# Two chunks of each feed-forward input projection as seven block products, on one Trainium2 core

## The chip, the cores and the metric

The kernel runs on one core of one Trainium2 chip. Its time is the device time of one execution in microseconds (us). Five engines work side by side, each with its own queue in order: PE multiplies matrices (PEld is the loading of its stationary operand), ACT (ScalarE), DVE (VectorE) and POOL (GpSimd) work element by element, SP issues the DMAs. PE writes to PSUM, eight banks of 128 x 512 floats; all other tiles lie in SBUF.

## What is computed

A trunk of two layers over 256 tokens of width 1024. Each layer is a feed-forward part (FFN), a token mixer and a second FFN, so there are four FFNs in the kernel. The change is in these:

```python
def swiglu_ffn(h, w_in, w_out):
    gate, up = jnp.split(h @ w_in, 2, axis=-1)        # w_in 1024 x 5632
    return (jax.nn.silu(gate) * up) @ w_out           # w_out 2816 x 1024

f = swiglu_ffn(rmsnorm(x, ffn1_norm_pre[i]), ffn1_w_in[i], ffn1_w_out[i])
x = x + 0.5 * rmsnorm(f, ffn1_norm_post[i])
```

The mixer between the FFNs (gated DeltaNet beside a causal convolution, with its own projections) is not touched.

## The kernel before, in words

**Products in three parts.** Every operand of a large product is kept as two float32r tiles, a high part `hi` and the rest `lo`, and `mm3` (L588) makes a product of three matmuls: high by high, high by low, low by high, all into one PSUM bank. Each matmul has a 128 x 128 stationary block of activations and 512 columns of weights.

**The weight stream.** `Stream` (L247) takes the weights in pieces of 128 x 1024 floats, 512 KB each. For each piece SP brings a `raw` tile (4 buffers), ACT copies it to `whi` (`high`, L276) and DVE or POOL makes `wlo` as raw minus whi (`low`, L280). `whi` and `wlo` have RING = 8 buffers each, so the preparation is at most eight pieces ahead of PE; `done` (L324) gives a buffer back when PE has used it and loads the next piece. In the FFNs all lows are DVE's; the set POOL (L75) names those of the mixer that GpSimd makes.

**The input projection** of an FFN, `proj_in` (L594), goes over 11 chunks of 512 columns: 256 gate columns and the 256 up columns that belong to them. A chunk is four pieces; each piece holds two of the eight 128-row steps of the inner dimension. For each of the two blocks of 128 tokens (tb 0, tb 1) a chunk takes 8 x 3 matmuls, 48 for the chunk, in two PSUM banks of tag `mm` (4 in all). At the start of an FFN (except the very first) chunks 0 and 1 are first done for tb 0 alone, while tb 1 is still being normalized.

**After a chunk**, `ev` (L699) takes the banks: ACT does the silu of the gate half, DVE multiplies by the up half. `fin` (L707) adds the job "ffn": two DVE transposes, four DMAs to DRAM, one DMA back, then ACT's high part and POOL's low part of the tile `act`, the operand of the output projection.

**The output projection**, `proj_out` (L655), has 22 steps of one piece each, 12 matmuls per piece, into four `mm` banks (two token blocks, two halves of 512 columns). The steps go by twos: two for tb 0, then the same two for tb 1. The last RING steps are finished first for tb 0, so that its normalization (`post`, L573, and `pre`, L449) runs beside tb 1.

**Order of the work.** PE runs in program order. `Lanes.tick` (L212) is called after every three matmuls or so and starts the next steps of the jobs, each after so many ticks as DELAY (L45) says. In the mixer the queues of DVE, POOL and ACT are put in the order of the program (`in_order`, `in_step`); in the FFNs of this kernel they are not, and the scheduler orders them by priorities. `Clocked` (L97) keeps an estimate of each engine's time while the program is written.

Of the kernel before, what the change touches and what calls it, by code (L numbers as in the profile page):

```python
# [76 lines left out]
CFG = dict(stat=1000, conv=50, ev=300, tok=4, st=4, post=-800, pre=1000, fin=None, turn=100, tokens=-100, glu=100, dec=200, dts=500, kt=300, vt=0, qt=50, inv=1000, sim=100, merge=-400, scan=50, norm=-800, onorm=-100, yt=-400, w=50, tails=4, ahead=1.5, lag=6, free=3, aheadp=3, lag2=3, bias=2, held=1)  # L77
# [4 lines left out]
        "yt0": "yt", "yt1": "yt"}  # L82
# [78 lines left out]
class Held:  # L161


    def __init__(self, eng, pe):
        self.eng, self.pe, self.tc = eng, pe, None

    def __getattr__(self, name):
        op = getattr(self.eng, name)

        def issue(*a, **k):  # L170
            r = op(*a, **k)  # L171
            if self.tc is not None:
                behind(self.tc, getattr(r, "ins", r), self.pe.last)
            return r
        return issue


class Lanes:
# [33 lines left out]
    def tick(self):  # L212
# [3 lines left out]
        if self.stream is not None:  # L216
            self.stream.tick()
# [28 lines left out]

class Stream:  # L247


    def __init__(self, tc, nc, pool, pieces, side, act, vec, gp):  # L250
        self.tc = tc
        self.act, self.vec, self.gp = act, vec, gp
# [4 lines left out]
        self.lanes, self.his, self.lows, self.still = None, [], [], True  # L257

# [4 lines left out]

    def load_one(self, parts=1):
        nc, src = self.nc, self.pieces[self.nload]
        i, n = self.nload, src.shape[-1]
        raw = self.pool.tile([P, D], F32, name="raw", tag="raw", bufs=4)
        hi = self.pool.tile([P, D], F32R, name="whi", tag="whi", bufs=RING)
        lo = self.pool.tile([P, D], F32R, name="wlo", tag="wlo", bufs=RING)
        for k in range(parts):  # L270
            c = slice(k * n // parts, (k + 1) * n // parts)
            nc.sync.dma_start(raw[:, c], src[:, c])
        self.loaded.append((hi, lo))
        self.nload += 1

        def high(c):  # L276
            with prio(self.tc, "w"):
                self.act.copy(hi[:, c], raw[:, c])
# [45 lines left out]
    def done(self):  # L324
        self.loaded[self.taken] = None
        self.taken += 1
        if not self.still:
            self.load()
# [1190 lines left out]
```

## Time and profile before

| what | value |
|---|---|
| time, median of 3 runs | 1345.21 us (1344.38 to 1346.62) |
| the profiled execution's own time | 1346.66 us |
| its span, first to last instruction | 1344.9 us |
| DMA | 273.77 MB, mean 204 GB/s |
| instructions | 20532 |

The page of the profile gives the busy time of each engine, then the span in 40 slices (one digit is a tenth of busy time), the DMA queues, the chain of work that ended last, and groups of instructions: line, engine, operation, output <- inputs, shapes, count, then busy us and mean ns of one, then the idle time just before them and what ended it. Lines 144, 171 and 124 are those of helpers that issue all of PE's, ACT's and DVE's or POOL's instructions, so groups are told apart by their tiles: `whi<-raw` is the high part of a weight piece, `wlo<-raw,whi` its low part, `ag<-mm` the gate, `way<-ag` the transposes, `act<-way` the parts of the output projection's operand, `xt<-tr` the splitting of the transposed input.

### The profile page before, as it was taken

The page shows a single profiled execution, that of the slowest core. Times are in us where ns is not written, and L with a number is a line of the kernel's source. Part 1 is how long each engine was busy: PE and PEld are TensorE (multiplying, and loading weights), DVE is VectorE, ACT ScalarE, POOL GpSimd, SP SyncE. Part 2 cuts the span into 40 slices and gives each one's busy share as a digit, 9 for nine tenths or more (in the row PEclk, how much of TensorE's full clock was granted, in tenths as well). Part 3 has the DMA queues.
Part 4 walks back from the last instruction along what each step waited for, and adds up shares of the span by engine and source line. Part 5 has one row for each costly group of instructions (what it writes and reads, how often), then busy time and mean ns, then how long its engine had stood idle before and what let it go on. Part 6 is the DMA issues. An engine that isn't in the chain of part 4 may idle for free.

```text
span 1344.9 us, 20532 instructions
## 1 busy us (share of the span) xinstructions
PE 1321.2 (98%) x7419; PEld 1120.4 (83%) x7419; DVE 931.6 (69%) x1592; ACT 731.8 (54%) x1175; POOL 451.2 (34%) x376
## 2 busy tenths in 40 slices
PE   9999999999999999999999999999999999999998
PEld 6888878998787878888888888799977878888886
DVE  6676455999975776665476654569999666766653
ACT  7555447676556545554455543577656564555541
POOL 0121016798853201111001110277997531011110
PEclk9999999999999999999999999999999999999999
DMA  8878746553643667776467776475536436477760
GB/s 280 280 238 254 260 159 199 179 187 120 192 155 126 232 212 235 253 260 220 151 228 268 258 253 190 129 236 168 183 122 206 154 133 233 158 267 261 260 210 34
DMA packets 115653, 273.77 MB, mean 204 GB/s; under 512 B 24768, under 2 KB 48352, under 8 KB 115552
## 3 DMA queue, kind: packets, MB, share of 16 engines
q1 hardware_dynamic: 115264, 272.40, 60.9%
q8 instruction: 58, 0.95, 0.3%
q14 instruction: 43, 0.35, 0.1%
q10 hardware_dynamic: 288, 0.07, 0.0%
HBM read 256.68 MB, written 15.75 MB: 203 GB/s over the span
## 4 chain that ended last, share of the span: by engine, by line
PE 77%; DVE 10%; POOL 3%; ACT 3%; issue 3%; DMA 3%; SPq 0%; POOLq 0%; DVEq 0%; ACTq 0%
PE mm L144 72%; DVE cacc L124 3%; PE gd L144 3%; DVE c L124 3%; DVE wlo L124 2%; POOL wlo L124 2%; PE tr L150 2%; DMA raw<-mw 2%; ACT whi L171 1%; DVE at L124 1%; POOL rk L124 1%; ACT dt L171 1%; DMA raw<-w2i 0%; DMA x<-x 0%; DMA raw<-w1i 0%
## 5 line engine op out<-in xcount | busy, mean ns | idle before, releaser
L144 PE MATMUL mm<-whi,xt 128*128 128x512 f32 (+1 forms) x2048 | 647.4, 391 | 4.2 <-ACT qT L171 2.2
L171 ACT CAST whi<-raw 128x1024 fp32r<-128x1024 f32 (+2 forms) x448 | 458.7, 1035 | 318.9 <-PE mm L144 177.8
L124 DVE TENSOR_TENSOR wlo<-raw,whi 128x1024 fp32r<-128x1024 f32 (+1 forms) x340 | 424.3, 1262 | 190.0 <-ACT whi L171 183.7
L144 PEld LDWEIGHTS mm<-whi,xt 128*128 128x128 f32 x2048 | 382.2, 188 | 85.0 <-DVE xt L124 3.1
L144 PE MATMUL mm<-wlo,xt 128*128 128x512 f32 (+1 forms) x1024 | 396.2, 387 | 0.1
L124 POOL TENSOR_TENSOR wlo<-raw,whi 128x1024 fp32r<-128x1024 f32 (+1 forms) x108 | 254.1, 2371 | 143.7 <-ACT whi L171 142.9
L144 PEld LDWEIGHTS mm<-wlo,xt 128*128 128x128 f32 x1024 | 192.7, 188 | 37.2 <-DVE wlo L124 0.8
L144 PE MATMUL mm<-whi,act 128*128 128x512 f32 x704 | 218.1, 390 | 0.0
L124 POOL TENSOR_TENSOR act<-way,act 128x512 fp32r<-128x512 f32 x44 | 81.2, 1845 | 393.8 <-ACT act L171 393.8
L124 DVE SCALAR_TENSOR_TENSOR cacc<-hT,pc,cacc 128x254 f32<-128x254 f32 (+28 forms) x464 | 179.3, 465 | 0.2
L144 PE MATMUL mm<-xt,whi 128*128 128x256 f32 x960 | 175.5, 285 | 0.8 <-ACT qT L171 0.6
L144 PEld LDWEIGHTS mm<-whi,act 128*128 128x128 f32 x704 | 132.2, 188 | 27.3
L144 PEld LDWEIGHTS mm<-xt,whi 128*128 128x128 f32 x960 | 149.4, 192 | 1.9 <-ACT qT L171 0.9
L144 PE MATMUL mm<-wlo,act 128*128 128x512 f32 x352 | 136.9, 389 | 0.0
L144 PE MATMUL mm<-xt,wlo 128*128 128x256 f32 x480 | 135.8, 283 | 0.0
L171 ACT ACTIVATE ag<-mm,rstd 128x256 f32<-128x256 f32 x88 | 41.8, 475 | 106.6 <-PE mm L144 76.3
L144 PEld LDWEIGHTS mm<-xt,wlo 128*128 128x128 f32 x480 | 92.0, 192 | 0.0
L124 DVE SCALAR_TENSOR_TENSOR ag<-mm,rstd,ag 128x256 f32<-128x256 f32 x88 | 42.4, 481 | 62.3 <-ACT ag L171 62.1
L144 PEld LDWEIGHTS mm<-wlo,act 128*128 128x128 f32 x352 | 66.1, 188 | 13.7
L124 POOL TENSOR_TENSOR rpost<-ss,exp 128x1 f32<-128x1 f32 x12 | 6.5, 541 | 194.0 <-DVE ss L124 194.0
L171 ACT ACTIVATE jk<-mm 128x512 f32<-128x512 f32 x24 | 14.4, 598 | 59.6 <-PE mm L144 59.6
L124 DVE SCALAR_TENSOR_TENSOR c<-mm,pc,c 128x255 f32<-128x255 f32 (+2 forms) x108 | 43.6, 473 | 2.6 <-ACT c L171 2.6
(187 smaller groups left out, 1139.2 us busy)
## 6 DMA issues: line engine op xcount, KB each, us to landing
raw<-mw SPq DMA_DIRECT2D x168, 512.0 KB, 3.7
raw<-w2i SPq DMA_DIRECT2D x88, 512.0 KB, 4.7
raw<-w1i SPq DMA_DIRECT2D x84, 512.0 KB, 4.8
raw<-w1o SPq DMA_DIRECT2D x44, 512.0 KB, 4.4
raw<-w2o SPq DMA_DIRECT2D x44, 512.0 KB, 4.2
way<-way SPq DMA_DIRECT2D x176, 64.0 KB, 1.8
way<-way SPq DMA_DIRECT2D x44, 256.0 KB, 4.6
wbc<-feat SPq DMA_DIRECT2D x13, 512.0 KB, 5.5
```

The costliest lines, as they stand in the source:

```text
L124: r = op(out, *a, **k)
L144: r = self.eng.matmul(o, w, x, **k)
L150: r = self.eng.transpose(*a)
L171: r = op(*a, **k)
```

## The change

In each of the four FFNs the chunks 9 and 10 (UNITS) are no longer two times 48 matmuls but one unit. With the tokens as two block rows, the inner dimension as two halves and the two chunks as two block columns, the product is a 2 x 2 by 2 x 2 block product, and it is formed by Winograd's variant of Strassen's method: seven block products in place of eight, each of 4 x 3 matmuls (`product`), so 84 matmuls.

- The right operands of the seven products, in the order FORMS, are three raw blocks of the weights (11, 21, 22) and four sums of blocks, t1 to t4 (SUMS), two pieces each, so the unit reads 14 pieces from the ring where the two chunks read 8. The 8 raw pieces come by DMA as before; the two of block 11 and the two of block 21 lie in slots of their own, the others in the four raw buffers. t1, t2 and t4 are formed by DVE in place in four PSUM banks (the three of tag `tr` and the one of `cacc`), t3 in place over block 11. Each sum and each part of a sum's piece is done in two instructions of 512 columns. NEEDS tells what must be done before the next sum overwrites a place.
- The left operands are three raw blocks of the activations and four sums of them (`early`): 12 DVE and 4 ACT instructions of 128 x 512 in each FFN, started 57 ticks ("forms") after `early`, which is called when the first banks have been evicted (in the very first FFN: at the start of chunk 1).
- `unit` accumulates on in three banks q, r and s: ACT copies q or r away (`kept`) while the next product goes to another bank, and three of the four gates begin with a DVE addition of such a copy (job "gates").
- From `early` on to the tenth step of the output projection the queues of DVE, POOL and ACT are in the program's order. `Stream` then plans the stream itself: `bring` issues DMAs, `best` and `pump` pick for each engine the next sum, high or low by estimated clocks, up to one us (beat) beyond PE's estimated time; sums may be made 14 pieces (far) beyond the ring. POOL gets a low only if it ends in time and at least three operations that read PSUM are ready for DVE (apart).
- The low part of `act` moves from POOL to DVE; chunks 0 and 1, and 9 and 10, go through one set of turning DMAs each; the `way` tiles have two slots in place of four.
- Some DELAYs differ: "first" (the jobs of the kernel's start), "pre0", "pre1", "ffn". The row of the post-norm's weights is loaded at the tenth step of the output projection.

The core of the diff:

```diff
+    "first": (0, 1, 0, 0, 0, 0, 0), "forms": (57, 0, 6, 0, 1), "gate": (0, 1), "gates": (0, 1, 1),
+    "ffn": (3, 2, 8, 12, 0), "pre0": (12, 12, 10, 0, 21, 2), "pre1": (14, 43, 4, 12, 8), "yt0": (10, 0, 10, 10, 26),
...
+UNITS = 4*((9,),)
+
+FORMS = ("11", "t1", "t2", "21", "t3", "22", "t4")
+
+SUMS = {"t1": ("12", "11"), "t2": ("22", "t1"), "t3": ("t2", "11"), "t4": ("21", "t2")}
+
+NEEDS = {"t1": (), "t2": (("t1", "low"),), "t3": (("t2", "summed"), ("11", "low")), "t4": (("t2", "low"), ("t3", "summed"))}
+
+USERS = {"12": (("t1", "summed"),), "22": (("22", "low"), ("t2", "summed")), "11": (("t3", "low"),), "21": (("21", "low"), ("t4", "summed"))}
...
+
+    raws = {(b, j): Raw(src(int(b[0]) - 1, int(b[1]) - 1, j), key(b, j)) for b in ("11", "12", "22", "21") for j in range(2)}
+    ps = {}
+    for j in range(2):
+        banks = Banks(lambda k, j=j: new(j and k))
+        at = {"t1": banks, "t2": banks, "t4": banks, "t3": raws["11", j]}
+        p = {f: Piece(at[f] if f in at else raws[f, j], f, 1.36) for f in FORMS}
+        for f in FORMS:
+            ps[f, j] = p[f]
+            p[f].group = list(raws.values())
+            if f in SUMS:
+                p[f].ins = [banks if b[0] == "t" else raws[b, j] for b in SUMS[f]]
+                p[f].needs = [(p[g], did) for g, did in NEEDS[f]]
+                p[f].parts = [slice(0, 512), slice(512, D)]
+        for b, users in USERS.items():
+            raws[b, j].users = [(p[f], did) for f, did in users]
+    return [ps[f, j] for f in FORMS for j in range(2)]
+
...
+    def bring(self, now):
+        while self.raws:
+            raw = self.raws[0]
+            self.out = [r for r in self.out if not r.free(now)]
+            if raw.first > self.taken + RING + CFG["far"]:
+                break
+            if sum(r.key == raw.key for r in self.out) >= (4 if raw.key is None else 1):
+                break
+            if self.fetch > now + CFG["depth"]:
+                break
+            self.raws.pop(0)
+            raw.tile = self.fresh() if raw.key is None else self.held(raw.key)
+            self.nc.sync.dma_start(raw.tile[:, :raw.src.shape[-1]], raw.src)
+            self.fetch = max(self.fetch, now) + 1.9
+            raw.landed = self.fetch + CFG["land"]
+            self.out.append(raw)
...
+    def shared(self, p, kind):
+        return p.form == "t1" if kind == "sum" else kind == "low" and (p.form is None or p.form not in ("t1", "t2", "t4"))
...
+    def best(self, eng, now, until, ahead):
+        found, due, apart = None, self.begun, 0
+        at = max(eng.at, now)
+        for p in self.pieces[self.taken:self.nload + ahead]:
+            kind, t = self.job(p)
+            dead = due
+            due += p.use
+            if t is None or (kind == "high") != (eng is self.act):
+                continue
+            shared = self.shared(p, kind)
+            if eng is self.gp:
+                if not shared:
+                    apart += t + 0.1 < at + 1.5
+                if kind == "sum" or not shared:
+                    continue
+            t = max(at, t + 0.1, self.lock if shared else 0.0)
+            if t >= until:
+                continue
+            if eng is self.gp and t + 2.4 > dead - CFG["slack"]:
+                continue
+            if found is None or t < found[0] - 0.2:
+                found = (t, p, kind)
+            if t <= at + 0.2 and eng is not self.gp:
+                break
+        return found if eng is not self.gp or apart >= CFG["apart"] else None
...
+    def issue(self, eng, t, p, kind):
+        eng.at = t
+        if self.shared(p, kind):
+            self.lock = t + (2.25 if eng is self.gp else 1.08)
...
+    def pump(self, until=None):
+        now = self.pe.at
+        until = now + CFG["beat"] if until is None else until
+        while True:
+            self.bring(now)
+            can = [(found, k) for k, eng in enumerate((self.act, self.vec, self.gp))
+                   for found in [self.best(eng, now, until, CFG["far"])] if found is not None]
+            if not can:
+                break
+            (t, p, kind), k = min(can, key=lambda c: (c[0][0], c[1]))
+            self.issue((self.act, self.vec, self.gp)[k], t, p, kind)
...
+    def homes(c):
+        return [*range(c, 11), *((13, 17) if c > 4 else (17, 13))][:8]
...
+        if first and early:
+            early()
         for c in range(len(chunks)):
+            if c in units:
+                unit(c)
+            if c in units or c - 1 in units:
+                continue
+            if c == 1 and not first and early:
+                lanes.finish(due[1])
+                early()
...
+            if kt == 10 and leave:
+                leave()
...
+            job = lanes.add("gate", steps())
+            if st.planned:
+                lanes.step(job)
+            else:
+                lanes.finish(job)
...
+                ways.append(slot(11 + len(ways) % 2, [P, 2, 512], name="way"))
+                way, n = ways[-1], len(cs)
...
-                    W.tensor_tensor(lo, src, hi.bitcast(F32), op=ALU.subtract)
+                for h, c in enumerate(cs):
+                    src = way[:, h].rearrange("p (i b t) -> p b i t", i=4, b=4)
+                    hi, lo = (act[c][:, n].rearrange("p k b (i t) -> p (k b) i t", i=4) for n in range(2))
+                    with prio(tc, "fin"):
+                        S.copy(hi, src)
+                        V.tensor_tensor(lo, src, hi.bitcast(F32), op=ALU.subtract)
+                    yield
...
+        def fin_one(c):
+            if c:
+                fin(*((0, 1) if c == 1 else (c,)))
...
+            def steps():
+                p21, p11, p12 = ps_tr(), ps_tr(), ps_tr()
+                whole(p21, 1, 0)
+                whole(a[:, 0], 1, 1)
+                V.tensor_tensor(a[:, 1], p21, a[:, 0], op=ALU.add)
+                high(1, a[:, 1])
+                yield
+                whole(p11, 0, 0)
+                V.tensor_tensor(b[:, 0], a[:, 1], p11, op=ALU.subtract)
+                high(2, b[:, 0])
+                low(1, a[:, 1])
+                yield
+                V.tensor_tensor(b[:, 1], a[:, 0], b[:, 0], op=ALU.subtract)
+                high(3, b[:, 1])
+                low(2, b[:, 0])
+                yield
+                whole(p12, 0, 1)
+                V.tensor_tensor(a[:, 0], p12, b[:, 0], op=ALU.subtract)
+                high(4, a[:, 0])
+                low(3, b[:, 1])
+                yield
+                low(4, a[:, 0])
+
+            for eng in (V, W, S):
+                eng.in_order(tc)
+            st.plan(lanes)
+            sums["job"] = lanes.add("forms", steps())
...
+        def unit(c):
+            lanes.finish(sums["job"])
+
+            def product(ps, f, start):
+                for j in range(2):
+                    w = st.peek(0)
+                    for k in range(2):
+                        kt = 2 * j + k
+                        ks = slice(512 * k, 512 * k + 512)
+                        mm3(ps, f[:, 0, kt, :], f[:, 1, kt, :], w[0][:, ks], w[1][:, ks], start and kt == 0, kt == 3,
+                            skip_group_check=True)
+                        lanes.tick()
+                    st.done()
+
...
+            def gate(c, tb, ps, more=None):
+                if more is None:
+                    ev(c, tb, ps)
+                    return
+
+                def steps():
+                    a = gated[c, tb] = tokt("ag", [P, 2, 256])
+                    with prio(tc, "ev"):
+                        V.tensor_tensor(a.rearrange("p a b -> p (a b)"), ps, more, op=ALU.add)
+                    yield
+                    with prio(tc, "ev"):
+                        S.activation(a[:, 0, :], a[:, 0, :], AF.Silu, scale=xt[tb][1])
+                    yield
+                    with prio(tc, "ev"):
+                        V.scalar_tensor_tensor(a[:, 1, :], a[:, 1, :], xt[tb][1], a[:, 0, :], op0=ALU.mult, op1=ALU.mult)
+                lanes.step(lanes.add("gates", steps()))
+
+            q, r = ps_mm(), ps_mm()
+            s1, s5 = (work.tile([P, 512], F32, name="sm", tag=f"state{i}", bufs=1) for i in range(2))
+            s2 = slot(14, [P, 512], name="s2")
+            product(q, blk[0, 0], True)
+            kept(q, s1)
+            product(r, sums[1], True)
+            kept(r, s5)
+            product(q, sums[2], False)
+            kept(q, s2)
+            s = ps_mm()
+            product(s, blk[0, 1], True)
+            gate(c, 0, s, s1)
+            product(q, sums[3], False)
+            gate(c + 1, 1, q, s5)
+            product(r, sums[4], False)
+            gate(c + 1, 0, r, s2)
+            product(q, blk[1, 1], False)
+            gate(c, 1, q)
+            fin(c, c + 1)
...
+        def leave():
+            lanes.flush()
+            wbc.append(load_feat(l, wpost, 17))
+            st.plan(None)
+            for eng in (V, W, S):
+                eng.in_order(None)
```

More of the change, by code (lines that the diff above doesn't have):

```diff
@@ L216, in tick @@
         if self.stream is not None:
+            self.stream.act.at = max(self.stream.act.at, self.pe.at)
+        if self.stream is not None:
             self.stream.tick()
@@ L244, in prio, with __init__, free, part @@
     return nullcontext() if key is None or not CFG[key] else tc.high_priority(offset=CFG[key])
+class Raw:
+    def __init__(self, src, key=None):
+        self.src, self.key, self.tile, self.landed, self.users = src, key, None, None, []
+    def free(self, now):
+        return all(getattr(p, did) is not None and getattr(p, did) <= now for p, did in self.users)
+    def part(self, c):
+        return self.tile[:, c]
+class Banks:
+    def __init__(self, new):
+        self.new, self.tiles, self.landed, self.key = new, None, 0.0, "psum"
+    def part(self, c):
+        if self.tiles is None:
+            self.tiles = [self.new(k) for k in range(2)]
+        return self.tiles[c.start // 512][:, c.start % 512:c.stop - c.start // 512 * 512]
+class Piece:
+    def __init__(self, raw, form=None, use=2.72):
+        self.raw, self.form, self.use, self.n = raw, form, use, 0
+        self.hi = self.lo = self.summed = self.high = self.low = None
+        self.ins = self.needs = ()
+        self.parts = [slice(0, D)]
+        self.group = []
+def unit_pieces(src, key, new):
+    raws = {(b, j): Raw(src(int(b[0]) - 1, int(b[1]) - 1, j), key(b, j)) for b in ("11", "12", "22", "21") for j in range(2)}
[14 more added lines that the diff above has]
+    return [ps[f, j] for f in FORMS for j in range(2)]
 class Stream:
-    def __init__(self, tc, nc, pool, pieces, side, act, vec, gp):
+    def __init__(self, tc, nc, pool, pieces, side, act, vec, gp, pe, held):
         self.tc = tc
-        self.act, self.vec, self.gp = act, vec, gp
+        self.act, self.vec, self.gp, self.pe, self.held = act, vec, gp, pe, held
         self.side = side
@@ L317, in in_step, with plan @@
         self.lanes = lanes
+    def plan(self, lanes):
+        if lanes is not None:
+            self.planned, self.lanes, lanes.stream, self.begun = True, lanes, self, self.pe.at
+            self.raws = []
+            for p in self.pieces[self.nload:self.nload + 120]:
+                for raw in p.group:
+                    if raw not in self.raws:
+                        raw.first = p.n
+                        self.raws.append(raw)
+            self.out = []
+        else:
+            for p in self.pieces[self.taken:self.nload]:
+                self.force(p)
+            self.planned, self.lanes.stream, self.lanes = False, None, None
@@ new lines, in job, with latest @@
+    def job(self, p):
+        def latest(times):
+            return None if any(t is None for t in times) else max(times, default=0.0)
+        if p.form in SUMS and p.summed is None:
+            return "sum", latest([getattr(q, did) for q, did in p.needs] + [r.landed for r in p.ins])
+        if p.hi is None:
+            return None, None
+        if p.high is None:
+            return "high", p.summed if p.form in SUMS else p.raw.landed
+        if p.low is None:
+            return "low", p.high
+        return None, None
@@ new lines, in issue @@
+    def issue(self, eng, t, p, kind):
+        eng.at = t
+        if self.shared(p, kind):
+            self.lock = t + (2.25 if eng is self.gp else 1.08)
+        n = D if p.form else p.raw.src.shape[-1]
+        for c in p.parts if p.form else [slice(0, n)]:
+            if kind == "sum":
+                a, b = (r.part(c) for r in p.ins)
+                with prio(self.tc, "w"):
+                    eng.tensor_tensor(p.raw.part(c), a, b, op=ALU.subtract)
+            elif kind == "high":
+                self.to_high(p, c)
+            else:
+                self.to_low(p, c, eng)
+        setattr(p, {"sum": "summed"}.get(kind, kind), eng.at)
@@ L319, in peek, with force @@
+    def force(self, p):
+        until = self.pe.at
+        while p.low is None:
+            until += 0.5
+            if until > self.pe.at + 100:
+                raise RuntimeError(f"stuck {p.n} {p.form}")
+            self.bring(until)
+            self.pump(until)
     def peek(self, i):
-        if self.lanes is not None:
+        if self.planned:
+            self.force(self.pieces[self.taken + i])
+        elif self.lanes is not None:
             self.tick(self.taken + i)
@@ L326, in done @@
         self.taken += 1
+        self.begun = self.pe.at
         if not self.still:
@@ L722, in steps @@
                 yield
[L723 to L731 removed]
+                for h, c in enumerate(cs):
+                    src = way[:, h].rearrange("p (i b t) -> p b i t", i=4, b=4)
[4 more added lines that the diff above has]
+                    yield
@@ L733, in lhs @@
+        proj_in(xt, [(512, 2)] * 11, ev, fin_one, first, units=units, unit=unit, early=early)
+        wbc = []
+        def leave():
[4 more added lines that the diff above has]
+                eng.in_order(None)
         def lhs(kt, tb):
```

202 lines of the change are left out of this document (135 added, 67 removed), and 20 rows, old and new, of the table DELAY.

## The prediction

> **What bounds the kernel now.** I read the page first: engine shares, then the slices of PE and its clock.
>
> ```profile
> span 1344.9 us, 20532 instructions
> PE 1321.2 (98%) x7419; PEld 1120.4 (83%) x7419; DVE 931.6 (69%) x1592; ACT 731.8 (54%) x1175; POOL 451.2 (34%) x376
> PE   9999999999999999999999999999999999999998
> PEclk9999999999999999999999999999999999999999
> ```
>
> PE is busy in every slice and at full clock; the other engines have room. But a busy PE can hide slow matmuls, so next comes the chain of waits in order of time, and then one projection as a stretch of its own.
>
> ```profile
> 14.47 163.56 PE mm L144 x720
> 504.92 157.89 PE mm L144 x696
> 686.88 162.75 PE mm L144 x718
> 1169.42 168.77 PE mm L144 x744
> ```
> ```profile
> core 0: us, PE busy (x) PEld busy (x) DVE busy (x) ACT busy (x) POOL busy (x), PEclk, DMA share, GB/s
> 504.90:613.70 108.80, 108.80 (x482) 89.93 (x481) 71.21 (x85) 58.23 (x75) 16.94 (x10) 1.00 0.75 250
> 613.70:662.80 49.10, 49.10 (x218) 40.70 (x217) 21.33 (x20) 17.80 (x20) 3.63 (x2) 1.00 0.57 185
> ```
>
> In each FFN the chain is one unbroken run of matmuls: 163.56/720 = 227.2 ns each in the first, 157.89/696 = 226.9 ns in the second, 226.7 and 226.8 in the others. The stretches are ten chunks of the second FFN's input projection and the start of its output projection: PE busy 108.80 of 108.80 us, no gap. So inside an FFN every matmul taken away is worth 226.9 ns, as long as the others keep up. DVE is the next engine: 71.21/108.80 = 65% in the input projection, 21.33/49.10 = 43% in the output projection. The durations there:
>
> ```profile
> L144 PE MATMUL mm<-whi,xt 128*128 128x512 f32 x320 | 98.8, 390 | 0.0
> L144 PE MATMUL mm<-wlo,xt 128*128 128x512 f32 x160 | 62.3, 389 | 0.0
> L124 DVE TENSOR_TENSOR wlo<-raw,whi 128x1024 fp32r<-128x1024 f32 x43 | 54.8, 1285 | 23.3 <-ACT whi L171 22.8
> L171 ACT CAST whi<-raw 128x1024 fp32r<-128x1024 f32 x43 | 44.8, 1050 | 29.0 <-PE mm L144 16.1 <-DMA raw<-w2i 12.6 <-ACT whi L171 0.3
> L124 POOL TENSOR_TENSOR act<-way,act 128x512 fp32r<-128x512 f32 x9 | 16.4, 1822 | 83.2 <-ACT act L171 83.2
> L124 DVE SCALAR_TENSOR_TENSOR ag<-mm,rstd,ag 128x256 f32<-128x256 f32 x20 | 9.6, 481 | 13.6 <-ACT ag L171 13.6
> L171 ACT ACTIVATE ag<-mm,rstd 128x256 f32<-128x256 f32 x20 | 9.5, 475 | 21.0 <-PE mm L144 19.0 <-DVE ag L124 1.9
> L124 DVE STREAM_TRANSPOSE way<-ag 128x256 f32<-128x256 f32 x19 | 8.0, 436 | 0.6
> L171 ACT CAST act<-way 128x512 fp32r<-128x512 f32 x9 | 5.5, 616 | 0.0
> L124 DVE TENSOR_TENSOR xt<-tr,xt 128x512 fp32r<-128x512 f32 x2 | 1.4, 692 | 2.6 <-ACT xt L171 2.5
> L171 ACT CAST xt<-tr 128x512 fp32r<-128x512 f32 x1 | 0.6, 586 | 0.0
> ```
> ```profile
> L171 ACT ACTIVATE jk<-mm 128x512 f32<-128x512 f32 x24 | 14.4, 598 | 59.6 <-PE mm L144 59.6
> L124 POOL TENSOR_TENSOR wlo<-raw,whi 128x1024 fp32r<-128x1024 f32 (+1 forms) x108 | 254.1, 2371 | 143.7 <-ACT whi L171 142.9
> ```
>
> 320 + 160 = 480 matmuls, as ten chunks of 48 should be. ACT waits mostly for PE (a full ring), so preparation runs ahead of use.
>
> **Part 1: the matmuls.** Two chunks are 96 matmuls, the unit 84. Over four FFNs 48 fall away: 48 x 226.9 ns = 10.9 us, all on the path. The Trainium skill ("TensorE: Matmul & The Clock Gate", Back-to-back issue gap) gives N/2.4 + 2.5 ns for a single matmul of N columns, 215.8 ns here, and about 131 ns in a sustained stream; by these the saving would be 10.4 or 6.3 us. The trace's sustained stream has 226.9 ns, so I keep 10.9.
>
> **Part 2: the sums of x.** Per FFN 12 DVE instructions of 128 x 512 and 4 ACT copies, nearest rows `xt<-tr` (692 and 586 ns): 8.3 us DVE, 2.3 us ACT. `early` is followed by 48 ticks up to the end of chunk 3, so tick 57 falls in chunk 4, five chunks or 54 us before the unit. DVE idles (108.80 - 71.21)/10 = 3.8 us per chunk, and the ring holds eight pieces, 8 x 12 x 0.2269 = 21.8 us of PE. Cost zero; without that cover it would be 8.3 us per FFN.
>
> **Part 3: the low of `act` on DVE.** 11 x 0.69 = 7.6 us more DVE per FFN, 20 us (11 x 1.822) less POOL. POOL's part was not free for DVE:
>
> ```profile
> 624.47 1.23 DVE L124 TENSOR_TENSOR wlo<-raw,whi 128x1024 fp32r<-128x1024 f32 x1 [2.85 <-ACT whi L171]
> 625.94 1.99 DVE L124 TENSOR_TENSOR wlo<-raw,whi 128x1024 fp32r<-128x1024 f32 x1 [0.24 <-ACT whi L171]
> ```
> ```profile
> 625.04 1.81 POOL L124 TENSOR_TENSOR act<-way,act 128x512 fp32r<-128x512 f32 x1 [7.30 <-ACT act L171]
> ```
>
> A low alone takes 1.23 us; the one issued while POOL works takes 1.99 and ends 1.08 after POOL does (625.94 + 1.99 against 625.04 + 1.81). So DVE gains 0.76 where they met and pays 0.69: zero. Fewer turning DMAs (two sets saved per FFN, of the 5 issues that each has) are also zero: SP is on no path here.
>
> **Part 4: DVE through the unit.** This is where a loss can come. The unit lasts 84 x 0.2269 = 19.1 us and uses a piece every 1.36 us; the output projection needs its first two pieces at 19.1 and 20.4. DVE must by then have made, counted from the unit's start: lows of one piece of 21, two of 22 and two of the output projection, 5 x 1.23 = 6.2; lows of t3 and t4 in halves, 8 x 0.69 = 5.5; chunk 8's two gates, two transposes and `act` low, 0.96 + 0.87 + 0.69 = 2.5; three additions and three multiplications of the unit's gates, 2.1 + 1.4 = 3.5. Together 17.7 of 20.4 us. In the two chunks before it (21.8 us): 16 half sums of t1 to t4, 11.1; lows of 11, 11, 21 (3.7) and of t1, t2 (8 x 0.69 = 5.5); chunk 7's 2.5. That is 22.8, one us too many, of which some lies earlier (t1 needs only raw pieces) and POOL may take a low. All in all 40.5 of 42.2 us, 96%, with nothing lost between instructions. I put the wait for the output projection's pieces at 0 to 1.0 us per FFN and take 0.5, half way. ACT over the unit: eight copies of 1.05, eight halves of 0.59, three `kept` of 0.60, five silus of 0.475, one 0.62: 17.9 of 19.1 us. It is tight too, but its copies are needed only eight pieces later.
>
> **Part 5: banks handed on.** Product 7 goes on in q, which DVE's addition for the fifth product must have read first; one product, 2.7 us, lies between. The plan lets DVE be 1.0 us ahead of PE plus one low begun (1.23), then the addition 0.69: 2.9. Bounds 0 and 1.2 (if DVE is a further us behind its plan); I take 0.2, near the lower end. Its last gate reads q after PE has left:
>
> ```profile
> 613.44 0.39 PE L144 MATMUL mm<-whi,xt 128*128 128x512 f32 x1
> 613.67 0.39 PE L144 MATMUL mm<-whi,act 128*128 128x512 f32 x1
> 613.92 0.47 ACT L171 ACTIVATE ag<-mm,rstd 128x256 f32<-128x256 f32 x1 [0.88 <-DVE ag L124]
> 614.42 0.48 DVE L124 SCALAR_TENSOR_TENSOR ag<-mm,rstd,ag 128x256 f32<-128x256 f32 x1
> ```
>
> Here, at the same place before, the bank is free at 614.90, 1.23 us after the output projection's first matmul. The four accumulators start at its matmuls 1, 4, 13 and 16. The three other banks are free long before; if q goes to the last accumulator it is needed after 15 x 0.2269 = 3.4 us. The latest case, DVE's multiplication behind a tick (0.68), the us of plan and a low (1.23), ends at 0.68 + 1.0 + 1.23 + 0.48 = 3.4. Cost zero; the other order is a rival.
>
> **Part 6: the start.** The "first" job's steps now follow each other every tick, so x's last quarter is transposed at tick 5, not 8: nine matmuls, 2.0 us, earlier than here.
>
> ```profile
> 7.45 0.44 PE L150 MATMUL tr<-cst,x 128*128 128x128 f32 x2 [0.75 <-DMA x<-x]
> 13.87 0.60 PE L150 MATMUL tr<-cst,x 128*128 128x128 f32 x4
> 7.43 0.33 SPq L491 DMA_DIRECT2D x<-x  x1
> ```
> ```profile
> x<-x SPq DMA_DIRECT2D x2, 256.0 KB, 5.1
> ```
>
> That is 11.8, but the quarter's DMA, issued at 7.43, lands about 12.5: up to 0.7 us of waiting. An earlier wait of the same kind (0.75) stands in the row. Bounds -0.3 and 1.4 (twice that, should the DMA be issued later); I take 0.4. The new "pre0" and "pre1" move one step by one or two ticks and leave the other to be forced at the same place: zero, within 1 us over the whole kernel.
>
> **The sum** against the profiled execution, 1346.66 us (span 1344.9 and 1.8 around it): -10.9 + 4 x (0.5 + 0.2) + 0.4 = -7.7, so 1339.0 us. That execution lies 1.45 us above the median of the runs, 1345.21; on the median the forecast is 1337.5 us.
>
> **Rivals.** (a) *q goes to the second accumulator*, needed after 0.68 us. At best the bank is free 1.23 us after, as above, a stall of 0.55; at worst 3.4, a stall of 2.7. Middle 1.6 per FFN: 1337.5 + 6.5 = 1344.0. For it: tags rotate, and q is the oldest of four. Against: its release is the latest of the four. 0.14.
>
> (b) *DVE becomes the bound: slower.* The place is the 42.2 us of part 4, of which 96% are spoken for. The sums form a chain in place (sum, copy, low, next sum), and in an ordered queue one late copy holds all behind it. If each of the operations takes 13% longer or waits as much, DVE needs 45.8, PE waits 3.6 us per FFN: 1345.21 - 10.9 + 14.4 + 0.4 = 1349.1. The point from which it decides is 10.5/4 = 2.6 us of waiting per FFN. For it: DVE's 22.8 us of waiting for `whi` among 43 lows. Against: those waits come from a full ring, and at 614.42 DVE starts without a gap. 0.13.
>
> (c) *POOL's help costs.* A low on POOL takes 2.37 us, and a DVE low that meets it waits until it ends, as at 625.94. Two such lows in the unit block 4.7 us and save 2.5, a loss of 2.3 per FFN less what is left of the margin (42.2 - 40.5 - 0.5 = 1.2): 1337.5 + 4.4 = 1341.9. The Trainium skill ("SBUF — State Buffer", SBUF: two separate sides) calls it an exclusive lock held for the whole instruction; the rows agree, with 1.99 us against 1.23. Against: the plan gives POOL a low only beside three operations that read PSUM. 0.08.
>
> **How the numbers follow.** The forecast (gain 5 to 11 us) has 0.65. A measurement of this kernel can tell about 0.2%, 2.7 us, from no change: 1342.5 to 1347.9 is "same". Faster: 0.65, about 0.05 of (a), 0.06 of (c): 0.76. Same: 0.09 of (a), 0.02 of (c), 0.01 of (b): 0.12. Slower: the rest of (b), 0.12. The range: below, all waits at their lower ends, 10.9 + 0.3, and 0.5 of the uncertain steps at the FFNs' ends: 1333.5. Above it takes in (c) and most of (a): 1345.0.
>
> **What would show it.** Right: matmuls fewer by 48; 84 of them between chunk 8 and `mm<-whi,act`, in about 19.3 us; PE's waits there for `wlo` or `ag` below 1 us; the clock at 1.00. Wrong: starts of PE delayed by `wlo<-sum` or by `ag` at the unit's end (b, a), DVE lows of 2 us and more within the unit (c), gaps in chunks 1 to 8, or a first FFN that reaches its steady run much later than 14.47.

## The result, and the profile after

The changed kernel takes 1337.82 us (median of 6 runs, 1336.74 to 1339.61), the kernel before 1345.47 us beside it (6 runs, 1344.38 to 1347.87). The ratio is 0.994, with a 95% interval of 0.9928 to 0.9953: faster by 7.65 us or 0.6%, forecast 7.7. The profiled execution after took 1336.74 us (span 1335.0).

First the page after, the same lines that were read of before.

```profile
span 1335.0 us, 20602 instructions
PE 1310.3 (98%) x7371; PEld 1112.0 (83%) x7371; DVE 1032.8 (77%) x1816; ACT 771.1 (58%) x1259; POOL 369.1 (28%) x332
PEclk9999999999999999999999999999999999999999
```

PE has 7419 - 7371 = 48 matmuls fewer, and the granted clock stays at 0.9 or more in every slice (0.999 on the mean). DVE has 224 instructions and 101.2 us more; POOL has 44 fewer, the lows of `act`. Next the chain of waits of after, in order of time (start, length, what, how many).

```profile
12.73 162.78 PE mm L154 x717
...
501.47 163.24 PE mm L154 x720
...
788.55 52.57 PE mm L154 x231
...
1269.85 58.57 PE mm L154 x257
```

The first FFN and its projections are still one run of matmuls, 162.78/717 = 227.0 ns each, and the second is too. In the third and fourth the run is broken early in the output projection. The place in the third is this; PE first, then DVE:

```profile
786.15 0.39 PE L154 MATMUL mm<-whi,act 128*128 128x512 f32 x1
787.29 0.61 PE L154 MATMUL mm<-whi,act 128*128 128x512 f32 x2
788.55 0.50 PE L154 MATMUL mm<-wlo,act 128*128 128x512 f32 x1 [0.65 <-DVE wlo L134]
...
785.61 0.69 DVE L134 TENSOR_TENSOR ag<-mm,s 128x512 f32<-128x512 f32 x1
786.21 0.69 DVE L134 TENSOR_TENSOR act<-way,act 128x512 fp32r<-128x512 f32 x1
787.28 1.22 DVE L134 TENSOR_TENSOR wlo<-raw,whi 128x1024 fp32r<-128x1024 f32 x1
788.42 0.48 DVE L134 SCALAR_TENSOR_TENSOR ag<-mm,rstd,ag 128x256 f32<-128x256 f32 x1
```

The output projection begins at 786.15. Its second piece needs a low that DVE starts at 787.28; PE waits 0.65 us for it and goes on at 788.55. The last gate, which reads bank q, runs from 788.42 to 788.90, 2.75 us after the projection began, and PE does not wait for it. How full DVE is shows in the 42.2 us that the prediction counted (two chunks, the unit and one piece; busy time of each engine, granted clock, DMA share):

```profile
core 0: us, PE busy (x) PEld busy (x) DVE busy (x) ACT busy (x) POOL busy (x), PEclk, DMA share, GB/s
745.30:787.50 42.20, 42.20 (x187) 34.94 (x187) 41.12 (x66) 29.56 (x47) 0.00 (x0) 1.00 0.57 187
```

DVE is busy for 41.12 of 42.20 us, 97%; all of its idle time lies before 746.38, and from there to the output projection it has no gap. From the first matmul of each projection in the two timelines, what became shorter and longer:

| stretch | before, us | after, us | difference |
|---|---|---|---|
| first FFN, input projection | 123.52 | 120.77 | -2.75 |
| first FFN, output projection | 61.02 | 60.87 | -0.15 |
| first layer's mixer, with its projections | 301.90 | 301.77 | -0.13 |
| second FFN, input projection | 121.85 | 118.62 | -3.23 |
| second FFN, output projection | 60.69 | 60.69 | 0 |
| third FFN, input projection | 121.28 | 118.04 | -3.24 |
| third FFN, output projection | 61.04 | 61.68 | +0.64 |
| second layer's mixer, with its projections | 300.37 | 301.46 | +1.09 |
| fourth FFN, input projection | 121.13 | 118.47 | -2.66 |
| fourth FFN, output projection, to the last matmul | 59.61 | 60.25 | +0.64 |

The four input projections give 11.9 us: 10.9 for the 48 matmuls, and 1.0 because the short gaps at the start of the second and third FFN are smaller in this execution. The output projections take 1.1 back and the mixers, which the change does not touch, another 1.0: 9.8 of the 9.9 us between the two spans. The medians lie 7.65 us apart because before's profiled execution is 1.2 us above its median here and after's 1.1 below.

### The profile page after: what moved, and what is told of

Read it like the earlier page. It is cut to its first block, busy times and chain, and to the rows that moved or that the text cites. A ratio compares the mean times of both kernels' runs of the same rounds, so it can differ in the third digit from the quotient of the medians.

```text
span 1335.0 us, 20602 instructions
## 1 busy us (share of the span) xinstructions
PE 1310.3 (98%) x7371; PEld 1112.0 (83%) x7371; DVE 1032.8 (77%) x1816; ACT 771.1 (58%) x1259; POOL 369.1 (28%) x332
## 4 chain that ended last, share of the span: by engine, by line
PE 66%; DVE 19%; DMA 6%; ACT 5%; issue 3%; POOL 1%; SPq 0%; DVEq 0%; POOLq 0%; ACTq 0%
PE mm L154 61%; DVE wlo L134 6%; DVE cacc L134 4%; PE gd L154 3%; DMA raw<-w2i 2%; DVE c L134 2%; DMA raw<-mw 2%; ACT whi L189 2%; PE tr L160 2%; DVE sum L134 1%; DVE ag L134 1%; DMA x<-x 1%; DVE at L134 1%; DMA raw<-w1i 1%; ACT dt L189 1%
## 5 line engine op out<-in xcount | busy, mean ns | idle before, releaser
L154 PE MATMUL mm<-whi,xt 128*128 128x512 f32 (+1 forms) x1888 | 598.8, 391 | 3.4 <-ACT qT L189 2.2
L189 ACT CAST whi<-raw 128x1024 fp32r<-128x1024 f32 (+1 forms) x424 | 434.6, 1035 | 282.5 <-PE mm L154 63.3
L134 DVE TENSOR_TENSOR wlo<-raw,whi 128x1024 fp32r<-128x1024 f32 (+1 forms) x316 | 375.7, 1211 | 108.8 <-ACT whi L189 106.3
L154 PEld LDWEIGHTS mm<-whi,xt 128*128 128x128 f32 x1888 | 352.8, 188 | 76.7 <-ACT qT L189 3.0
L154 PE MATMUL mm<-wlo,xt 128*128 128x512 f32 (+1 forms) x944 | 364.9, 387 | 0.0
L154 PEld LDWEIGHTS mm<-wlo,xt 128*128 128x128 f32 x944 | 177.7, 188 | 33.1
L189 ACT ACTIVATE ag<-mm,rstd 128x256 f32<-128x256 f32 x76 | 33.8, 471 | 31.6 <-PE mm L154 31.5
L134 DVE TENSOR_TENSOR act<-way,act 128x512 fp32r<-128x512 f32 x44 | 30.2, 686 | 21.9 <-ACT act L189 21.9
L134 DVE SCALAR_TENSOR_TENSOR ag<-mm,rstd,ag 128x256 f32<-128x256 f32 x76 | 33.9, 477 | 13.5 <-ACT ag L189 13.5
```

What stands on the lines that cost most here:

```text
L134: r = op(out, *a, **k)
L154: r = self.eng.matmul(o, w, x, **k)
L189: r = op(out, *a, **k)
```

## The experiments

Each kernel is the changed one with the edit shown. The ratio is to the kernel before on the same chip; there the kernel before took 1345.0 to 1345.6 us in all of them, so the times can be set beside the 1337.82 of after. By the intervals, a difference of 2 or 3 us between two of these kernels is known to about 2 us.

| run | us | ratio, 95% interval |
|---|---|---|
| no_units | 1345.89 | 1.0004 (0.9996 to 1.0013) |
| old_delays | 1338.42 | 0.9948 (0.9936 to 0.9960) |
| sums_of_x_at_40 | 1339.62 | 0.9951 (0.9935 to 0.9968) |
| sums_of_x_at_80 | 1358.04 | 1.0100 (1.0085 to 1.0115) |
| sums_of_x_at_90 | 1369.85 | 1.0175 (1.0156 to 1.0193) |
| act_low_on_pool | 1340.83 | 0.9967 (0.9955 to 0.9979) |
| pool_helps | 1349.00 | 1.0027 (1.0014 to 1.0040) |
| spare_dve_work | 1366.84 | 1.0164 (1.0149 to 1.0179) |
| spare_dve_one | 1357.18 | 1.0092 (1.0077 to 1.0107) |
| spare_one_same_order | 1340.35 | 0.9968 (0.9955 to 0.9981) |
| units_4_and_9 | 1502.41 | 1.1161 (1.1136 to 1.1186) |
| units_7_and_9 | 1458.06 | one run, no interval |

The theory was that the gain is the 48 matmuls less the waits in a DVE that is nearly full. The rivals: that the planned queues or the new delays bring part of it, and that DVE has more room than the ledger says, or less.

**Is it the matmuls?** All chunks plain, but planned queues, delays, sums of x and the moved lows kept (the sums are made and not used):

```diff
-UNITS = 4*((9,),)
+UNITS = 4*((),)
```

> The changed kernel with no unit: chunks 9 and 10 as two chunks of 48 matmuls, all else (planned queues, sums of x, act lows on DVE, delays) as changed. Theory (the gain is the 48 matmuls, the rest is near zero): 48 x 0.227 = 10.9 us come back less the waits of the unit ends, which the trace puts at 1.4 us in all, so about 9.5 us above the changed kernel and 1.5 us above or below the time before: 1345 to 1348 us. Rival (the planned queues or the new delays carry a share of the gain): 1343 us or less.

1345.89 us, no different from before. So the whole gain, 1345.89 - 1337.82 = 8.1 us, comes with the units: 10.9 us of matmuls less 2.8 us. Of these 2.8 the traces show 1.8 in the output projections, which are longer by that much in after than in no_units; the rest is not located.

**The delays.**

```diff
-    "first": (0, 1, 0, 0, 0, 0, 0),
+    "first": (1, 1, 2, 2, 2, 2, 2),
...
-"pre0": (12, 12, 10, 0, 21, 2), "pre1": (14, 43, 4, 12, 8),
+"pre0": (10, 7, 8, 4, 5, 3), "pre1": (15, 16, 0, 13, 8),
```

> The changed kernel with the delays of first, pre0 and pre1 as before. Theory: each is worth under 1 us; the start is the same to 0.3 us, since both traces reach matmul 60 at 22.8 us, so 1336.5 to 1340 us. Rival (the delays are worth a part of the 7.7 us): 1341 us and above.

1338.42 us: not to be told from after. The 0.4 us of part 6 lies below what these runs can see.

**Where the sums of x may stand.** The first number is the tick at which they begin; three runs.

```diff
-"forms": (57, 0, 6, 0, 1)
+"forms": (90, 0, 6, 0, 1)
```

> The changed kernel with the sums of x started 90 ticks after early (chunk 6.6) in place of 57 (chunk 4.6). In the third FFN the changed kernel's DVE is busy 7.66 of 10.90 us in chunk 6 and without a gap from there on to the output projection. Theory (the sums' 12 instructions, 7.4 us at their spacing, cost nothing only where DVE idles): 4 to 6 us of them fall into the full stretch, PE waits at least as long in each unit, and what waits in order behind can make it two or three times as much, as with the spare additions: 16 to 60 us slower, 1354 to 1398 us. Rival (the eight pieces of the ring cover them, wherever they stand): 1337 to 1341 us.

> The sums of x begin at the 80th tick instead of the 57th, that is at the start of chunk 6 instead of in chunk 4; all else as after. Theory (zero cost only where DVE has room): DVE idles 3.2 us in chunk 6 and not at all from chunk 7 on, so of the 8.3 us of the sums some 5 are pushed into the full stretch: 5 us of lateness per FFN, 1337.8 + 8 to 30 us = 1346 to 1368, less than at 90 (1369.85). Rival (what hurt at 90 was the planned queues starting late, not DVE's room): already nearly as slow as at 90, over 1365.

> The sums of x begin at the 40th tick (chunk 3, as soon as the planned queues begin) instead of the 57th; all else as after. Theory (DVE has room in chunks 3 and 4 alike): no difference, 1336.5 to 1339.5 us. Rival (the place itself, with DVE's read of three PSUM banks and the ring's state at the change of queues, matters): slower by 2 us or more.

At 40, in chunk 3, the interval overlaps that of after: no difference that can be told. At 80 it is 1358.04, 20.2 us more than after. That is 5.1 per FFN on the mean, the size of what the expectation pushed past chunk 6, but the trace does not bear this out: the first FFN loses 10.5 us and the other three 3.1 to 3.5 each. At 90 it is 32.0 us more; the FFNs lose 7.4 to 8.4 us each, about the 8.3 us that the prediction gave as the price without cover. So where the sums stand matters, and 57 is far enough ahead. That DVE's room is the reason is argued, not shown: in both late runs the plan also puts instructions in another order (at 90 it gives POOL two lows per FFN as well), which, as the spare additions below show, can cost by itself; how much of the 20 and 32 us that is was not separated.

**The lows of `act`.**

```diff
-                        V.tensor_tensor(lo, src, hi.bitcast(F32), op=ALU.subtract)
+                        W.tensor_tensor(lo, src, hi.bitcast(F32), op=ALU.subtract)
```

> The changed kernel with the low part of act back on POOL. Theory (DVE is full only around the unit; moving 11 x 0.69 us off it and paying for the lock elsewhere is worth nothing): within 1.5 us of the changed kernel, 1336 to 1340 us, with DVE lows of about 2 us where they meet POOL. Rival (POOL's lock on DVE was part of what was saved): 3 us or more slower, 1341 us and above.

1340.83 us, 3.0 more than after, between the theory's 1340 and the rival's 1341. The third FFN in the timeline of this run (POOL, DVE and ACT, then PE):

```profile
777.88 1.48 POOL L134 TENSOR_TENSOR act<-way,act 128x512 fp32r<-128x512 f32 x1 [12.72 <-ACT act L189]
...
776.98 3.45 DVE L134 TENSOR_TENSOR wlo<-raw,whi 128x1024 fp32r<-128x1024 f32 x2
...
793.08 0.48 DVE L134 SCALAR_TENSOR_TENSOR ag<-mm,rstd,ag 128x256 f32<-128x256 f32 x1 [0.26 <-ACT ag L189]
...
791.63 1.05 ACT L189 CAST whi<-raw 128x1024 fp32r<-128x1024 f32 x1 [1.59 <-DMA raw<-w1o]
792.58 0.46 ACT L189 ACTIVATE ag<-mm,rstd 128x256 f32<-128x256 f32 x1
...
792.27 0.39 PE L154 MATMUL mm<-whi,act 128*128 128x512 f32 x1
793.62 0.50 PE L154 MATMUL mm<-whi,act 128*128 128x512 f32 x1 [0.97 <-DVE ag L134]
```

Two DVE lows beside POOL's take 3.45 us, where alone they would take at most 2 x 1.23. The last gate comes later, and PE stands at 792.27 until DVE has read bank q: 792.50 would have been its time, 15 matmuls (3.4 us) after 789.09, where this output projection begins. That is the fourth accumulator, so q goes to the last one, as the forecast had it. In after the same gate is done at 2.75 us; here the lateness uses up its cover. The lateness is not POOL's alone, though. The last gate waits for ACT's silu (792.58), and that stands behind the high part of a weight piece, which has waited 1.59 us for its DMA. In after the silu stands ahead of that high part:

```profile
786.75 0.46 ACT L189 ACTIVATE ag<-mm,rstd 128x256 f32<-128x256 f32 x1
789.45 1.06 ACT L189 CAST whi<-raw 128x1024 fp32r<-128x1024 f32 x1 [2.24 <-DMA raw<-w1o]
```

The plan has changed this order in all four FFNs, in two of them with such a wait for a DMA. How much of the 3.0 us is POOL's meeting with DVE's lows and how much the order was not separated.

**More help from POOL.** The plan gives POOL a low from one operation that reads PSUM on, instead of three; POOL then makes four lows per unit.

```diff
-apart=3
+apart=1
```

> The changed kernel with POOL allowed a low when one operation that reads PSUM is ready for DVE, not three: POOL then makes 4 lows around each unit, in the changed kernel none. Theory (DVE is the one engine without slack there, so what it sheds, 4 x 1.2 us, ends the waits of 0.1 to 0.8 us at the output projection's second piece): 0 to 3 us faster than the changed kernel, 1334.5 to 1338 us. Rival (POOL's lock stops DVE's lows from raw pieces for 2.4 us each, more than it saves): 2 us or more slower, 1340 us and above, with DVE lows of 2 us or more in the unit.

1349.0 us, 11.2 more than after; the theory of a help that gains fell. The second FFN, DVE and POOL, then PE:

```profile
598.36 6.89 DVE L134 TENSOR_TENSOR wlo<-held,whi 128x512 fp32r<-128x512 f32 x4
598.39 5.71 POOL L134 TENSOR_TENSOR wlo<-raw,whi 128x1024 fp32r<-128x1024 f32 x2 [1.36 <-ACT whi L189]
...
610.29 1.21 DVE L134 TENSOR_TENSOR wlo<-raw,whi 128x1024 fp32r<-128x1024 f32 x1
611.43 0.68 DVE L134 TENSOR_TENSOR ag<-mm,sm 128x512 f32<-128x512 f32 x1
...
608.91 0.39 PE L154 MATMUL mm<-whi,xs 128*128 128x512 f32 x1
612.16 0.80 PE L154 MATMUL mm<-whi,xt 128*128 128x512 f32 x1 [2.86 <-DVE ag L134]
612.75 0.63 PE L154 MATMUL mm<-wlo,xt 128*128 128x512 f32 x1
613.18 1.05 PE L154 MATMUL mm<-whi,xt 128*128 128x512 f32 x2
```
```profile
core 0: us, PE busy (x) PEld busy (x) DVE busy (x) ACT busy (x) POOL busy (x), PEclk, DMA share, GB/s
612.00:616.00 4.00, 3.84 (x10) 3.08 (x11) 4.00 (x7) 3.41 (x5) 0.00 (x0) 0.57 0.83 261
```

Four half lows on DVE take 6.89 us while POOL makes two whole ones in 5.71. The second and third of them last 2.90 and 2.89 us where one alone takes 0.69, and each ends 0.55 us after a low of POOL; the same stands in all four FFNs, 4.4 us each. The Trainium skill ("SBUF — State Buffer", SBUF: two separate sides) says that DVE with two inputs in SBUF and POOL take turns at one lock for whole instructions; these rows agree. POOL's other two lows (592.06 to 597.03) stand beside operations of DVE that read PSUM, and none of those is longer for it.

DVE's second addition, which reads bank q, comes late (611.43), and PE waits 2.86 us for it at the place of part 5, where product 7 starts in bank q. Here too the order has changed: the lows of the output projection's first two pieces (608.77 and 610.29) stand ahead of this addition, where in the third FFN of after the first of them (784.47) comes behind it (782.28). What of the 11.2 us is the lock and what the order was not separated.

After the gap the matmuls start 0.43 us apart (612.75, 613.18), at a granted clock of 0.57 over these 4 us, which is another 4 x (1 - 0.57) = 1.7 us lost. In this run each of the four FFNs has such a gap, 2.71 to 3.25 us from start to start, and at each of them the granted clock goes to 0.50 for 3.4 us; no slow matmuls follow the gaps of up to 1.66 us in act_low_on_pool. The Trainium skill ("TensorE: Matmul & The Clock Gate", What's actually happening) tells of half the clock after an idle window of about 3.4 us. The halving is in these rows, but shorter gaps were enough for it, and there the measurement decides.

Of this kernel's 11 runs (1345.25 to 1353.87 us, the traced one the longest) the four above 1350 us have a mean granted clock of 0.994 and the others 0.996 to 0.998, which suggests, without showing it, that the number of halvings differs from one execution to the next.

**Spare work on DVE.** One or four additions of 128x512, whose results go nowhere, in each unit:

```diff
+            both = slot(14, [P, 2, 512], name="s2")
+            s2 = both[:, 0]
+            def spare():
+                V.tensor_tensor(both[:, 1], s1, s1, op=ALU.add)
...
             kept(r, s5)
+            spare()
```

> The changed kernel with four additions of 128 x 512 more on DVE in each unit, of which nothing is used: 4 x 0.69 = 2.8 us per unit (2.4 us at the spacing of 0.60 us that the halves have). Theory (DVE is packed from 26 us before the output projection to 6 us after it, so each us more is a us of waiting at the output projection's first pieces): 4 x 2.4 = 9.6 us slower, 1346 to 1349 us, with PE waiting for lows 2.5 to 3.5 us at each unit's end. Rival (there is slack left, the wait of 0.8 us is only the order of two lows): at most 3 us slower, 1338 to 1341 us.

> The kernel after with one unused addition of 128x512 on DVE in each unit (behind the second product) instead of four; its result goes nowhere. Theory (lateness is paid as it is until a queue behind it starves): DVE is full in the unit, so 0.60 us more is 0.60 us more of waiting per FFN, 4 x 0.6 = 2.4 us: 1340.2 us, between 1338.5 and 1342. Rival (each addition costs what a quarter of the four cost, 29/4 = 7.2 us, because a late piece holds ACT and DVE behind it at once): 1345 us. If there is slack that I do not see: 1337.8.

Four cost 29.0 us, three times what was expected; one costs 19.4, more than either theory. I had explained the four by lateness that multiplies from queue to queue. That does not fit one addition costing two thirds of what four do. SP's queue in the second FFN shows what else changed: the kernel after, then spare_dve_one (with ACT and PE).

```profile
595.69 0.35 SPq L439 DMA_DIRECT2D raw<-w2o  x1
596.20 0.34 SPq L990 DMA_DIRECT2D way<-way  x1
598.01 0.33 SPq L439 DMA_DIRECT2D raw<-w2o  x1
602.18 0.81 SPq L587 DMA_DIRECT2D wbc<-feat  x2
```
```profile
605.36 0.35 SPq L587 DMA_DIRECT2D wbc<-feat  x1
605.89 0.34 SPq L990 DMA_DIRECT2D way<-way  x1
606.32 0.85 SPq L439 DMA_DIRECT2D raw<-w2o  x2
...
611.92 1.04 ACT L189 CAST whi<-raw 128x1024 fp32r<-128x1024 f32 x1 [4.34 <-DMA raw<-w2o]
...
614.55 0.79 PE L154 MATMUL mm<-wlo,xt 128*128 128x512 f32 x1 [3.61 <-DVE wlo L134]
```

Both have the same work for SP. In after, two pieces of the output projection are loaded ahead of `wbc`. In spare_dve_one the order has `wbc` first. That load waits for PE:

```profile
SPq L587 <- PE mm L154: 6.3, 1, 6.3
```

It waits 6.3 us, and the turning DMA and two raw pieces stand behind it. The pieces land late, ACT waits 4.34 us for one of them with a silu queued behind, DVE waits for ACT, and PE 3.61 us for DVE. The third FFN has the same change of order, and so have the second and third FFN of spare_dve_work. The plan counts the addition's time, and from there on the instructions come out in another order. So the addition was made without being counted:

```diff
             def spare():
+                at = V.at
                 V.tensor_tensor(both[:, 1], s1, s1, op=ALU.add)
+                V.at = at
```

> As spare_dve_one, one unused addition of 128x512 on DVE in each unit, but the plan does not count its time, so that every other instruction of DVE, ACT, POOL and SP stands in the same order as in the kernel after. In spare_dve_one the plan put the load of wbc ahead of the output projection's raw loads on SP in the second and third FFN (there it lost 8.7 and 6.2 us, in the first and fourth, where SP's order had stayed, about 3). Theory (what costs most is the changed order on SP, a wbc load that waits for PE with the raw loads behind it): the excess of FFN 2 and 3 goes, at most 3 us per FFN are left: 1340 to 1350 us, and 1340.2 if the 0.60 us is paid as it is. Rival (0.60 us of DVE's time does it alone): 1357 us, as in spare_dve_one.

```profile
599.37 0.35 SPq L439 DMA_DIRECT2D raw<-w2o  x1
599.89 0.34 SPq L990 DMA_DIRECT2D way<-way  x1
601.16 0.33 SPq L439 DMA_DIRECT2D raw<-w2o  x1
603.92 0.81 SPq L587 DMA_DIRECT2D wbc<-feat  x2
```

SP is back in the order of after, and so are all instructions of ACT, POOL and PE, and DVE's but for the four additions. The time is 1340.35 us: 2.5 more than after, where 4 x 0.60 = 2.4 was expected. The total hits, but not by 0.6 in each FFN: in the trace the four FFNs lose 1.5, 1.0, 0.2 and -0.2 us. Of the 19.4 us, 16.8 were the order and not DVE's time. That holds for the order of all queues together, since DVE's and ACT's also changed between the two; the `wbc` load is what the trace shows in the second FFN. In spare_dve_one the four FFNs lose 2.9, 8.6, 6.2 and 1.6 us, against after. In the first and the fourth SP's order up to the output projection is that of after, so the `wbc` load is not the only change that costs; and the fourth's loss is half of the 3 us that the expectation names.

**More units.** Chunks 4 and 5 as a unit as well, with the sums of x from tick 20; and, in another kernel, chunks 7 and 8.

```diff
-    "first": (0, 1, 0, 0, 0, 0, 0), "forms": (57, 0, 6, 0, 1),
+    "first": (0, 1, 0, 0, 0, 0, 0), "forms": (20, 0, 6, 0, 1),
...
-UNITS = 4*((9,),)
+UNITS = 4*((4, 9),)
```
```diff
-UNITS = 4*((9,),)
+UNITS = 4*((7, 9),)
```

> Two units in each FFN, for chunks 4, 5 and 9, 10, with the sums of x started at 20 ticks. Theory (PE gains 48 more matmuls, 10.9 us, but DVE needs 11.1 us of sums, 7.6 us of lows and 2 us of additions more per unit than two chunks do, and before chunk 4 there stand the sums of x and the quick chunks 0 and 1): waits of 3 to 8 us per FFN in the earlier unit, so 1 to 21 us slower than the changed kernel, 1339 to 1359 us. Rival (PE's matmuls alone set the time): 10.9 us faster, 1326 to 1328 us.

> Two units side by side in each FFN, chunks 7, 8 and 9, 10, the sums of x as in the changed kernel. Theory (a unit needs DVE for about 37 us, and two of them follow in 38 us of PE with one lead of 20 to 25 us before them, in which DVE has also the chunks): 10 us or more of waiting per FFN, 1366 us or more. Rival (PE's matmuls alone): 1326 to 1328 us.

Each has another 48 matmuls fewer, 7323, and is slower: 1502.41 and 1458.06 us. PE's waits in the first:

```profile
PE mm L154 <- DVE wlo L134: 52.2, 61, 3.8
PE mm L154 <- ACT whi L189: 46.5, 28, 2.1
```

That is 98.7 us, beside 1.0 for the low in after. The mean clock is 0.961, which by my estimate, (1 - 0.961) x 1503.5, is another 59 us. I had expected at most 1359 for units_4_and_9, by the room that DVE has in the early chunks. What part of the loss is work and what part order was not separated. The delays and the plan's margins were left at values made for one unit, so these runs show that a second unit does not come for nothing, not what a tuned one would take.

## Why the prediction was right, point by point

- **Part 1, 10.9 us of matmuls: right.** There are 48 fewer, and they are 227.0 ns apart in the first FFN after. no_units shows, to within 2 us, that the gain has no other source than the units. The table of stretches bears 10.9 out to about 1 us only. The two rates of the Trainium skill ("TensorE: Matmul & The Clock Gate", Back-to-back issue gap) would have given 10.4 or 6.3 us; the spacing of this stream is neither, and the measurement decides.
- **Part 2, sums of x at zero: right where they stand,** and no difference that can be told at tick 40. The price without cover, 8.3 us per FFN, stands beside 8.0 at tick 90, with the order changed there too.
- **Part 3, the low of `act` moved to DVE at zero: not borne out.** Moving it back costs 3.0 us, 0.75 per FFN, so the step "DVE gains 0.76 where they met and pays 0.69: zero" does not give the whole. What it left out shows at the last gate: a low that meets POOL, and a silu that the changed order puts behind a high part. Their shares are open.
- **Part 4, DVE's ledger: right in its total, and that by luck.** 40.5 of 42.2 us were counted, 41.12 measured. But the ledger left out 10 of the 66 instructions (three lows of raw pieces, three of `act`, two gates and two transposes of earlier chunks, about 7.6 us), and it added durations that overlap (0.09 us each, 5.6 us in all). What it was for, that DVE is full here and just in time, holds. The wait for the first pieces was put at 0.5 us per FFN; in the four FFNs the gaps in PE's timeline are 0.2, 0, 0.8 and 0.5, some 0.4 on the mean. spare_one_same_order shows how little slack there is: 0.60 us of work more in each FFN is 2.5 us of time more in all. It does not show it for each unit, as the first two FFNs paid more than 0.60 and the last two next to nothing.
- **Part 5, banks: right in kind.** PE has no wait for `ag` in after, where 0.2 per FFN was taken for product 7. q goes to the last accumulator.
- **Part 6, the start: 0.4 us taken, none paid.** PE does wait for x,

```profile
12.07 0.66 PE L160 MATMUL tr<-cst,x 128*128 128x128 f32 x4 [1.03 <-DMA x<-x]
```

but the 61st matmul of the projection starts at 22.80 us, before at 22.82: the wait takes the place of several shorter gaps that before has there. What sets the 22.8 us in both was not looked for.

By these sizes the sum is -10.9 + 4 x 0.4 = -9.3 us on the profiled execution, where -7.7 was forecast and the spans show -9.9. That the forecast on the median fell within 0.3 us of the measurement is luck in part: the small terms were 1.6 us too high, and by chance the two profiled executions lie on opposite sides of their medians, so that the gain on the medians is 2.2 us smaller than on the spans. The hit is closer than the working was.

The rivals: (a) fell, by the place of the gap in act_low_on_pool. (b) did not come, but spare_dve_one shows the way in that the prediction did not see: it took DVE's time as the danger and the order of the queues as given. (c) did not come because POOL makes no low in the FFNs. Made to, the block is real: two of POOL's four lows hold DVE up by 4.4 us, near the 4.7 that the prediction had for two. The price per FFN, 2.8 us, has the order and the clock in it as well.

## What to carry to other kernels

Where PE runs without a gap, a matmul saved is worth its spacing in the stream, as long as a ledger of the next engine over the stretch, not over the kernel, still closes (counted from start to start, as durations overlap). When an edit makes a planned schedule slower or faster than its own work can explain, compare the order of each queue with that of the kernel it came from, and repeat the edit with the order held: here 16.8 of 19.4 us were order, and the edits that moved lows between POOL and DVE cannot be read in full because this was not done for them. A load that waits for the bottleneck engine, as `wbc` does here, belongs behind the loads which that engine needs next.

## What the runs showed of the hardware

In the rows of after at 785.61 and 786.21, two DVE instructions of 128x512 last 0.69 us each and start 0.60 apart, so they overlap in the records: a sum of durations is too high by 0.09 us for each that follows another directly. Over the 66 instructions of part 4's stretch that comes to 5.6 us.

A gap in PE's work can halve its rate for a while. In pool_helps, with gaps of 2.71 to 3.25 us, the granted clock falls to 0.50 at the end of the gap or within 1.4 us of it, and stays there for 3.4 us, with matmuls 0.43 us apart. In spare_dve_one gaps of up to 2.12 us have no slow matmuls behind them when they stand alone. Near 2.5 us it can go either way: sums_of_x_at_90 has one gap of 2.49 or 2.50 us in each FFN, and only the one in the fourth is followed by it at once. A wait of that size costs more than it shows.
